# Decoder trunk on one core: the first slice of the lo half of each block's input in a tile of its own, 64 bytes further modulo 256

## The chip, the cores and the metric

The kernel runs on one core of one Trainium2 chip. The metric is the device time of one execution in microseconds (us). Before the change the median of three runs is 1512.07 us.

## What is computed

Two layers, each a SwiGLU feed-forward block (FFN), a token mixer with three branches, and a second FFN, on 256 tokens of width 1024. The reference, cut to its large products:

```python
for l in range(DEPTH):                       # DEPTH = 2
    g = norm_g[l]
    f = swiglu(rmsnorm(h, g[0]), w_ffn_gu[l, 0], w_ffn_down[l, 0])   # 1024 -> 2*2816 -> 1024
    h = h + 0.5 * rmsnorm(f, g[1])
    xn = rmsnorm(h, g[2])
    z = xn @ w_in[l]                         # 1024 -> 9224 columns
    ...
    merged = (gates[..., 0, :] * (y_m @ w_branch[l, 0])
              + gates[..., 1, :] * (y_s @ w_branch[l, 1])
              + gates[..., 2, :] * (y_x @ w_branch[l, 2]))
    y = merged @ w_out[l]
    h = h + rmsnorm(y, g[3])
    f = swiglu(rmsnorm(h, g[4]), w_ffn_gu[l, 1], w_ffn_down[l, 1])
    h = h + 0.5 * rmsnorm(f, g[5])
```

## The kernel before

**Products.** Every large product is taken to fp32 accuracy with three fp32r matmuls: each operand is split into a rounded half (hi, h) and the rest (lo, l), and hi·hi, hi·lo and lo·hi are summed in PSUM. `load_split` (L108 to L116) streams the weights: SyncE issues a DMA of 512 KB into `raw` (4 buffers), ScalarE casts `hi` (L114), VectorE subtracts to get `lo` (L115); `hi` and `lo` have 6 buffers each.

**The input of a block.** `split_x` (L174) makes the normalised, transposed input of an FFN or a mixer: for each of the 8 slices `kt` of 128 input channels ScalarE writes a slice of `xh` (L166) and VectorE a slice of `xl` (L167), each 128 x 256 (channels x tokens). It runs six times in the program, once for each of the two FFNs and the mixer of both layers. The slices lie one behind the other in one tile for `xh` and one for `xl`, so a slice starts 1024 bytes after the one before it.

**Transposed products.** `pair_T` (L191) loads 256 weight columns and makes two chains of matmuls (`cols_T`, `product`), each for 128 output columns:

```python
for (ah, al), (bh, bl) in terms:            # terms: kt = 0..7
    for u, v in ((ah, bh), (ah, bl), (al, bh)):
        nc.tensor.matmul(o, u, v, start=(i == 0), stop=(i == n - 1))   # L185
```

A chain is 24 matmuls: for each kt the weight slice hi with the moving operand `xh`, hi with `xl`, lo with `xh`; the weights are stationary (128 x 128), the input moves 256 columns. A call of `pair_T` is 48 matmuls at L185; the text calls it a block. The trace writes moving and stationary operand as `o<-xl,hi`. The program has 144 blocks with `xh` and `xl`: 22 in each of the four FFNs and 28 in each mixer. Blocks with other inputs (`ymh`/`yml`, `ysh`/`ysl`, `yxh`/`yxl` for the branches, `mh`/`ml` for the memory and the merged branches) are made by the same lines.

**Row products.** Where the result is wanted with tokens on the partitions, `rows_mm` (L198) takes the weights as the moving operand, 512 columns, and a 128 x 128 piece of the input as the stationary one (L203 hi, L204 lo, L205 with the lo half of the input). `group_rows` does this with `xh`/`xl`, `full_rows` for the FFN's second product with `hh`/`hl`; in the trace the moving operand again stands first (`acc<-hi,hh`, `o<-hi,xl`).

**Order.** An FFN goes over j = 0..10: two blocks with x (96 matmuls), then, from j = 1, two steps of the second product (`down`, 24 matmuls of 512 columns). The mixer mixes blocks, row products and small products by hand-written order. The order of the instructions on each engine is that in which the code is written.

**Where the tiles lie.** `TAGS` (L36) sets the size of each tile of the pool `act`, and so its start. `placed` (L118) takes a tile of that pool and views it as 8 slices. Bytes of SBUF in each partition, modulo 256: the weights `hi`, `lo` at 192, `xh` and `xl` at 128, `ymh`, `yml`, `ysh`, `ysl`, `yxh`, `yxl`, `mh`, `ml` at 128, `hh`, `hl` at 192.

Of the kernel before, what the change touches and what calls it, by code (L numbers as in the profile page):

```python
# [9 lines left out]
F32R = mybir.dt.float32r  # L10
# [4 lines left out]
P = 128  # L15
D = 1024
KT = D // P
S = 256
# [14 lines left out]
FREE = 4  # L33
BARE_TAIL = 3
BARE_FREE = 3
TAGS = {"xh": 2048, "xl": 2048, "qk": 2048, "vm": 2080, "vx": 2048, "yml": 2080, "kT": 2048, "ymh": 2048,  # L36
        "yxh": 2064, "yxl": 2096}
C_QK, C_V, C_O, C_I, C_F, C_U, C_SV, C_XQ, C_G = 0, 1024, 2048, 3072, 3076, 3080, 4104, 5128, 6152

# [2 lines left out]
def decoder_trunk(ctx: ExitStack, tc: tile.TileContext, x, mem, norm_g, w_ffn_gu, w_ffn_down, w_in, conv_w,  # L42
# [6 lines left out]
    act = ctx.enter_context(tc.tile_pool(name="act", bufs=1))  # L49
    tmp = ctx.enter_context(tc.tile_pool(name="tmp", bufs=2))  # L50
# [41 lines left out]
    def g_col(l, n, k):  # L92
        i = (l * 7 + n) * 8 + k
        return colA[:, i:i + 1]
# [13 lines left out]
    def load_split(src, a, b):  # L108
# [6 lines left out]
            nc.vector.tensor_tensor(out=lo, in0=raw, in1=hi.bitcast(F32), op=ALU.subtract)  # L115
        return hi, lo  # L116

    def placed(name, tag, dtype=F32R, at=0, n=KT * S):  # L118
        t = act.tile([P, TAGS[tag]], dtype, name=name, tag=tag)
        return t[:, at:at + n].rearrange("p (k s) -> p k s", s=S)  # L120
# [44 lines left out]
    def scaled_split(src, gain, hi, lo):  # L165
        last["act"] = nc.scalar.mul(hi, src, gain)  # L166
        last["dve"] = nc.vector.scalar_tensor_tensor(out=lo, in0=src, scalar=gain, in1=hi.bitcast(F32), op0=ALU.mult,  # L167
                                       op1=ALU.subtract)
# [3 lines left out]
        nc.vector.tensor_tensor(out=lo, in0=src, in1=hi.bitcast(F32), op=ALU.subtract)  # L172

    def split_x(l, n, pts):  # L174
        xh, xl = placed("xh", "xh"), placed("xl", "xl")
        for kt in range(KT):
            scaled_split(pts[kt // 2][:, kt % 2, :], g_col(l, n, kt), xh[:, kt, :], xl[:, kt, :])
        return xh, xl
# [56 lines left out]
    def boundary(accs, gb, mul, nxt, fill=(), lead=0):  # L235
# [28 lines left out]
        if lead:  # L264
            pts = new_pts()
            for tt in range(NT):
                transpose_in(xs[tt], tt, pts)
        xt = split_x(*nxt, pts)
        if not lead:
            hold[:] = [[]] * BARE_FREE + [[last["act"], last["dve"]]]  # L270
# [65 lines left out]
    def kv_parts(l):  # L336
        def start():
            mh, ml = placed("mh", "qk"), placed("ml", "vm")
            for kt in range(KT):
                scaled_split(memT[:, kt, :], g_col(l, 6, kt), mh[:, kt, :], ml[:, kt, :])  # L340
            vx = [act.tile([P, TAGS[t]], F32R, name="vx", tag=t)[:, 0:NT * D].rearrange("p (t d) -> p t d", d=D)
                  for t in ("vx", "yml")]
            kv[l] = ((mh, ml), [placed("kT", t) for t in ("kT", "ymh")], vx)

        def k_part(c):
            mt, kT, vx = kv[l]
            o = pair_T(w_mkv[l], c * 2 * P, mt)
            split(o, kT[0][:, 2 * c:2 * c + 2, :], kT[1][:, 2 * c:2 * c + 2, :])

        os_ = {}  # L350

        def v_quarter(c, q):
            mt, kT, vx = kv[l]
            os_[c] = group_rows(w_mkv[l], D + c * 512, mt, (q,), os_.get(c))
            if q == 3:
                for tt, o in enumerate(os_[c]):
                    split(o, vx[0][:, tt, c * 512:(c + 1) * 512], vx[1][:, tt, c * 512:(c + 1) * 512])

        return start, ([lambda c=c: k_part(c) for c in range(4)] +
                       [lambda c=c, q=q: v_quarter(c, q) for c in range(2) for q in range(4)])  # L360

    def mixer(l, xt, nxt, start=None, fill=(), lead=0):
# [55 lines left out]
        def attend(hd, pT):  # L418
# [7 lines left out]

        vm = act.tile([P, TAGS["vm"]], F32, name="vm", tag="vm")[:, 0:NT * NH * (DV + 1)].rearrange(
            "p (t h d) -> p t h d", t=NT, h=NH)
# [257 lines left out]
    transpose_in(xs, 1, pts)  # L686
    load_consts(rowA, colA, 112)
    xt = split_x(0, 0, pts)
    hold[:] = [[first], [], [last["act"], last["dve"]]]
    xt = ffn(0, 0, xt, (0, 2), {2: load_mem, 4: transpose_mem, 6: start0}, kv0, 3)  # L690
# [32 lines left out]
```

## Time and profile before

| | |
|---|---|
| median of 3 runs | 1512.07 us (1512.06 to 1513.64) |
| the profiled execution | 1514.27 us |
| its span in the trace | 1512.5 us |
| granted TensorE clock | 0.998 of 2.4 GHz |
| TensorE (PE) busy | 1493.2 us, 10870 matmuls |
| VectorE (DVE) busy | 929.3 us |
| ScalarE (ACT) busy | 749.0 us |
| DMA | 273.49 MB, 181 GB/s in the mean |

The span runs from the first to the last instruction that the profiler saw; the 1.8 us by which the execution is longer lie around it. A matmul's record in the trace is longer than the distance to the next one's start, since matmuls are pipelined: 276 to 283 ns stand in the record where the next starts after some 115 ns. What a matmul costs the engine is read from the distance of starts, or from the length of a piece of the chain of waits divided by its count.

### The profile page before, as it was taken

The numbers are of one execution on the slowest core, as the hardware profiler recorded it, in microseconds if no ns is written. First come the engines' busy times: TensorE is split into PE (matmuls) and PEld (weight loads), VectorE is DVE, ScalarE is ACT, GpSimd is POOL, SyncE is SP. The second block draws the span as 40 slices with busy tenths as digits, with TensorE's granted clock in tenths as the row PEclk, the third lists the DMA queues.
The fourth block names the chain that finished last, engine by engine and source line by source line (L and its number), as shares of the span: only waits on it lengthen the run. The fifth ranks groups of instructions, "written<-read, shape, count | busy, mean of one in ns | idle before, by whom it ended". The sixth has DMA issues, their size and how long they took to land.

```text
span 1512.5 us, 26330 instructions
## 1 busy us (share of the span) xinstructions
PE 1493.2 (99%) x10870; PEld 1410.2 (93%) x10870; DVE 929.3 (61%) x1319; ACT 749.0 (50%) x972; POOL 44.6 (3%) x77
## 2 busy tenths in 40 slices
PE   7999999999999999999999999999999999899998
PEld 7999998999999999999989999898998999799997
DVE  5564575777766567545465554576867665655454
ACT  6554464655444456444464444565544444454442
POOL 1000000000010000000000000000001000000000
PEclk9999999999999999999999999999999999999999
DMA  8666566455566565666656666655555656465662
GB/s 265 215 184 191 186 204 182 134 159 164 156 190 188 175 195 184 193 195 184 192 175 213 185 194 182 188 168 155 155 166 169 193 170 186 134 221 184 192 184 84
DMA packets 222169, 273.49 MB, mean 181 GB/s; under 512 B 12656, under 2 KB 194144, under 8 KB 222048
## 3 DMA queue, kind: packets, MB, share of 16 engines
q1 hardware_dynamic: 221920, 271.75, 59.4%
q8 instruction: 85, 1.39, 0.4%
q14 instruction: 36, 0.29, 0.1%
q10 hardware_dynamic: 128, 0.06, 0.0%
HBM read 270.72 MB, written 1.05 MB: 180 GB/s over the span
## 4 chain that ended last, share of the span: by engine, by line
PE 96%; DVE 2%; POOL 1%; DMA 0%; ACT 0%; issue 0%; SPq 0%; POOLq 0%; DVEq 0%; ACTq 0%
PE o L185 65%; PE acc L203 6%; PE acc L205 6%; PE acc L204 6%; PE o L203 3%; PE o L205 3%; PE o L204 3%; PE pts L159 1%; DMA raw<-in_w_ffn_gu_dram 0%; PE mx L647 0%; DVE lo L115 0%; PE zif L185 0%; POOL rs L142 0%; POOL rs L593 0%; ACT xh L166 0%
## 5 line engine op out<-in xcount | busy, mean ns | idle before, releaser
L115 DVE TENSOR_TENSOR lo<-raw,hi 128x1024 fp32r<-128x1024 f32 x504 | 614.0, 1222 | 493.0 <-ACT hi L114 483.6
L114 ACT CAST hi<-raw 128x1024 fp32r<-128x1024 f32 x504 | 527.4, 1050 | 600.9 <-PE o L185 279.4
L185 PE MATMUL o<-xh,hi 128*128 128x256 f32 x2304 | 650.6, 283 | 0.9 <-ACT xh L166 0.8
L185 PE MATMUL o<-xl,hi 128*128 128x256 f32 x2304 | 647.7, 281 | 0.4 <-DVE xl L167 0.3
L185 PE MATMUL o<-xh,lo 128*128 128x256 f32 x2304 | 647.1, 281 | 0.0
L185 PEld LDWEIGHTS o<-xh,lo 128*128 128x128 f32 x2304 | 440.2, 191 | 0.1
L185 PEld LDWEIGHTS o<-xh,hi 128*128 128x128 f32 x2304 | 434.6, 189 | 3.6 <-ACT xh L166 1.6
L185 PEld LDWEIGHTS o<-xl,hi 128*128 128x128 f32 x2304 | 435.1, 189 | 3.1 <-DVE xl L167 1.2
L203 PE MATMUL acc<-hi,hh 128*128 128x512 f32 x352 | 137.0, 389 | 0.0
L205 PE MATMUL acc<-hi,hl 128*128 128x512 f32 x352 | 136.8, 389 | 0.0
L204 PE MATMUL acc<-lo,hh 128*128 128x512 f32 x352 | 136.8, 389 | 0.0
L205 PEld LDWEIGHTS acc<-hi,hl 128*128 128x128 f32 x352 | 66.1, 188 | 13.9 <-DVE hl L172 0.2
L203 PEld LDWEIGHTS acc<-hi,hh 128*128 128x128 f32 x352 | 66.1, 188 | 12.5 <-ACT hh L171 0.3
L204 PEld LDWEIGHTS acc<-lo,hh 128*128 128x128 f32 x352 | 66.1, 188 | 12.2
L203 PE MATMUL o<-hi,xh 128*128 128x512 f32 x128 | 50.6, 395 | 0.0
L205 PE MATMUL o<-hi,xl 128*128 128x512 f32 x128 | 50.4, 394 | 0.0
L204 PE MATMUL o<-lo,xh 128*128 128x512 f32 x128 | 50.0, 391 | 0.0
L142 POOL TENSOR_TENSOR rs<-ms,mhalf 128x1 f32<-128x1 f32 x26 | 16.3, 627 | 1057.3 <-DVE ms L139 1057.3
L171 ACT CAST hh<-hf 128x512 fp32r<-128x512 f32 x44 | 27.4, 622 | 27.7 <-DVE hf L289 27.7
L185 PE MATMUL o<-yxh,hi 128*128 128x256 f32 x128 | 36.2, 283 | 0.0
L185 PE MATMUL o<-mh,hi 128*128 128x256 f32 x128 | 36.1, 282 | 0.0
L185 PE MATMUL o<-mh,lo 128*128 128x256 f32 x128 | 36.0, 281 | 0.0
(240 smaller groups left out, 1707.8 us busy)
## 6 DMA issues: line engine op xcount, KB each, us to landing
raw<-in_w_ffn_gu_dram SPq DMA_DIRECT2D x176, 512.0 KB, 4.7
raw<-in_w_in_dram SPq DMA_DIRECT2D x144, 512.0 KB, 3.7
raw<-in_w_ffn_down_dram SPq DMA_DIRECT2D x88, 512.0 KB, 4.4
raw<-in_w_branch_dram SPq DMA_DIRECT2D x48, 512.0 KB, 3.5
raw<-in_w_mkv_dram SPq DMA_DIRECT2D x32, 512.0 KB, 4.6
raw<-in_w_out_dram SPq DMA_DIRECT2D x16, 512.0 KB, 4.4
gb<-in_norm_g_dram SPq DMA_DIRECT2D x6, 512.0 KB, 4.4
h<-in_x_dram SPq DMA_DIRECT2D x4, 256.0 KB, 3.4
```

The costliest lines, as they stand in the source:

```text
L114: nc.scalar.copy(hi, raw)
L115: nc.vector.tensor_tensor(out=lo, in0=raw, in1=hi.bitcast(F32), op=ALU.subtract)
L142: nc.gpsimd.tensor_tensor(out=rs, in0=ms, in1=mhalf, op=ALU.pow)
L159: nc.tensor.transpose(out=pts[kt // 2][:, kt % 2, tt * P:(tt + 1) * P], in_=xs[kt // 4][:, kt % 4 * P:(kt % 4 + 1) * P], identity=ident)
L171: nc.scalar.copy(hi, src)
L185: nc.tensor.matmul(o, u, v, start=(i == 0), stop=(i == n - 1))
L203: nc.tensor.matmul(o, a, u, start=first, stop=False)
L204: nc.tensor.matmul(o, a, v, start=False, stop=False)
L205: nc.tensor.matmul(o, b, u, start=False, stop=last)
```

## The change

`split_x` takes its tiles from a new helper, `apart_x`. `xh` is as before. Of `xl` the slice kt = 0 goes into a tile `x0` of its own (pool `tmp`, one buffer), and the seven others into the `act` tile `xl`, which is smaller by one slice. `Slices` lets `cols_T` and `rows_mm` index both as before.

```diff
-TAGS = {"xh": 2048, "xl": 2048, "qk": 2048, ...
+TAGS = {"xh": 2048, "xl": 1792, "qk": 2048, ...
...
+    class Slices:
+        def __init__(self, parts):
+            self.parts = parts
+
+        def __getitem__(self, i):
+            return self.parts[i[1]][:, i[2]]
+
+    def apart_x():
+        zero = tmp.tile([P, S], F32R, name="x0", tag="x0", bufs=1)
+        rest = act.tile([P, TAGS["xl"]], F32R, name="xl", tag="xl")
+        return placed("xh", "xh"), Slices([zero] + [rest[:, k * S:(k + 1) * S] for k in range(KT - 1)])
...
     def split_x(l, n, pts):
-        xh, xl = placed("xh", "xh"), placed("xl", "xl")
+        xh, xl = apart_x()
```

The addresses that follow, in bytes in each partition, from the two built programs:

| tile | before | after | modulo 256 before | after |
|---|---|---|---|---|
| `xh` | 105088 | 112256 | 128 | 128 |
| `xl`, slices 1 to 7 | 113280 + 1024 kt | 105088 + 1024 (kt - 1) | 128 | 128 |
| `xl`, slice 0 (`x0`) | 113280 | 206016 | 128 | 192 |
| weights `hi`, `lo` | | unchanged | 192 | 192 |
| the other `act` tiles behind them | | 1024 lower | | unchanged |

No instruction is added, taken away or moved: with names and line numbers set aside the sequence of instructions of each engine, with what each waits for, is the same in both programs (PE 10798 rows, DVE 1321, ACT 907, POOL 82, SP 538). What changes is the address that one matmul in each chain of 24 reads its moving operand from (the second of the chain, `xl` of kt = 0), the address that 16 matmuls of `group_rows` load their stationary operand from, and the one that VectorE writes that slice to.

## Rows read from the trace of the kernel before

**Rows 1.** Page, parts 1 to 3: busy engines; granted clock by slice; share of DMA.
```profile
PE 1493.2 (99%) x10870; PEld 1410.2 (93%) x10870; DVE 929.3 (61%) x1319; ACT 749.0 (50%) x972; POOL 44.6 (3%) x77
...
PEclk9999999999999999999999999999999999999999
...
q1 hardware_dynamic: 221920, 271.75, 59.4%
```

**Rows 2.** Page, part 4: the chain that ended last, share by engine.
```profile
PE 96%; DVE 2%; POOL 1%; DMA 0%; ACT 0%; issue 0%; SPq 0%; POOLq 0%; DVEq 0%; ACTq 0%
```

**Rows 3.** What PE waited for: us in total, times, longest.
```profile
PE pts L159 <- DVE xs L153: 6.9, 3, 4.2
PE pt L89 <- DMA rowA<-in_norm_g_dram: 4.4, 1, 4.4
```

**Rows 4.** Page, part 5: groups by line: count, busy us, mean ns, idle before.
```profile
L115 DVE TENSOR_TENSOR lo<-raw,hi 128x1024 fp32r<-128x1024 f32 x504 | 614.0, 1222 | 493.0 <-ACT hi L114 483.6
...
L185 PE MATMUL o<-xl,hi 128*128 128x256 f32 x2304 | 647.7, 281 | 0.4 <-DVE xl L167 0.3
...
L203 PE MATMUL o<-hi,xh 128*128 128x512 f32 x128 | 50.6, 395 | 0.0
...
L204 PE MATMUL o<-lo,xh 128*128 128x512 f32 x128 | 50.0, 391 | 0.0
```

**Rows 5.** PE's groups by line, 434.84 to 450.6 us (first mixer).
```profile
L185 PE MATMUL o<-xl,hi 128*128 128x256 f32 x31 | 8.6, 276 | 0.0
...
L185 PE MATMUL o<-yml,hi 128*128 128x256 f32 x16 | 4.4, 276 | 0.0
```

**Rows 6.** The same view, 505.1 to 550.3 us (first mixer, later).
```profile
L185 PE MATMUL o<-xl,hi 128*128 128x256 f32 x64 | 18.0, 281 | 0.0
```

**Rows 7.** The chain of waits in order of time: start us, length us, what.
```profile
44.15 11.31 PE o L185 x96
60.89 11.31 PE o L185 x96
...
434.30 16.34 PE o L185 x144
...
505.10 45.23 PE o L185 x384
...
793.46 21.79 PE o L185 x192
...
1483.91 11.31 PE o L185 x96
```

**Rows 8.** Timeline of PE at 434 us, a block after a row product: start, record us.
```profile
434.14 0.28 PE L185 MATMUL o<-xh,hi 128*128 128x256 f32 x1
...
434.84 0.28 PE L185 MATMUL o<-xh,hi 128*128 128x256 f32 x1
...
435.18 0.28 PE L185 MATMUL o<-xh,hi 128*128 128x256 f32 x1
```

**Rows 9.** Timeline of PE at 44 us, the first block after a `down`.
```profile
43.98 0.28 PE L185 MATMUL o<-xh,hi 128*128 128x256 f32 x1
...
44.34 0.28 PE L185 MATMUL o<-xh,hi 128*128 128x256 f32 x1
```

**Rows 10.** Timeline of PE at 1344 us, the first `down` matmuls after a slow block.
```profile
1344.31 0.40 PE L203 MATMUL acc<-hi,hh 128*128 128x512 f32 x1
...
1345.01 0.39 PE L203 MATMUL acc<-hi,hh 128*128 128x512 f32 x1
...
1345.69 0.39 PE L203 MATMUL acc<-hi,hh 128*128 128x512 f32 x1
```

**Rows 11.** Timeline of PE at 38.5 us, the first `down` matmuls after a fast block.
```profile
38.53 0.39 PE L203 MATMUL acc<-hi,hh 128*128 128x512 f32 x1
...
39.22 0.39 PE L203 MATMUL acc<-hi,hh 128*128 128x512 f32 x1
...
39.90 0.39 PE L203 MATMUL acc<-hi,hh 128*128 128x512 f32 x1
```

More of the change, by code (lines that the diff above doesn't have):

```diff
@@ L35 @@
 BARE_FREE = 3
-TAGS = {"xh": 2048, "xl": 2048, "qk": 2048, "vm": 2080, "vx": 2048, "yml": 2080, "kT": 2048, "ymh": 2048,
+TAGS = {"xh": 2048, "xl": 1792, "qk": 2048, "vm": 2080, "vx": 2048, "yml": 2080, "kT": 2048, "ymh": 2048,
         "yxh": 2064, "yxl": 2096}
```

## The prediction

> **What bounds the kernel now.** I read the page's busy times first: TensorE is busy 99% of the span at full granted clock, VectorE 61%, ScalarE 50%, and the DMA engines are taken for 59% of it [rows 1]. Then the chain that ended last: 96% of it is TensorE [rows 2]. Then TensorE's waits: the two largest add up to 11.3 us, and both lie at a transpose, not in a product [rows 3]. So time can come only from the distance at which matmuls follow each other. L185 with `xh` and `xl` is the largest group, three forms of 2304 each [rows 4].
>
> Next I asked whether that distance is the same everywhere. It isn't. In the chain of waits, pieces of 96 matmuls without an interruption take 11.31 us, 117.8 ns each; there are 37 of exactly this length, from 44.15 to 1483.91 us, 36 of them with x [rows 7]. But 144 of the same matmuls take 16.34 us at 434.30, 113.5 ns each, and 192 at 793.46 take 21.79, also 113.5 [rows 7]. Grouped by line, the record of the same form is 276 ns in the one kind of stretch and 281 in the other [rows 5, 6]. Nothing waits in either, the clock is the same, the addresses are the same [rows 1, 5, 6]. The timeline shows how a pace starts. After a row product the block at 434.14 needs 0.70 us for its first six matmuls, unevenly, and from 434.84 three take 0.34 us, 113.3 ns each [rows 8]. The block at 43.98 takes 0.36 us for its first three [rows 9], evenly, and stays slow. A pace is kept through whole blocks and changes only where another kind of matmul comes between. Going through the program by starts I count, of the 144 x blocks, 120 slow, 2 half and half, 22 fast; of the `ym` and `ys` blocks, which follow x blocks, 14 slow and 2 fast.
>
> Of the entries into a block that begin unevenly, as at 434.14, I found eleven (around 96, 315, 324, 338, 434, 793, 993, 1056, 1066, 1080 and 1175 us), and all eleven settled at the fast pace within four to six matmuls. The slow pace was always entered without any unevenness. That is what the forecast rests on: slow looks like a stable beat that a disturbance ends.
>
> **The change, part by part.**
>
> *The instructions.* None is added or moved, so nothing new is issued, queued or waited for on any engine, SP's queue and POOL included. VectorE writes slice 0 with the same instruction to another address: nothing. The other `act` tiles move by 1024 bytes and keep their place modulo 256: nothing.
>
> *The second matmul of every chain* reads its moving operand at 192 modulo 256, where its stationary one lies too, instead of 128. The trace has no such matmul of 256 columns. The nearest rows are those where the kind of operand changes between neighbours: the first `down` matmul after a block, whose moving weights are at 192. At 1344.31 three of these take 0.70 us, against 0.68 for three a little later [rows 10]: the shift gives an uneven step, and then a settled pace. So I take it as a disturbance in each chain, 288 in all (144 blocks of two).
>
> *What a disturbance costs.* At 434.14 six matmuls take 0.70 us where the fast pace needs 0.68, so 0.02 us [rows 8]; the first three after 1344.31 lose 0.02 too [rows 10]. As bounds I take 0.01 and 0.045 us (nothing smaller shows in stamps of 10 ns; 0.045 is twice the rows). Taken: 0.025, so 288 x 0.025 = 7.2 us.
>
> *What it gives, if each chain then settles at the fast pace.* 117.8 - 113.3 = 4.5 ns a matmul. 122 slow blocks (the two halves counted as slow, which is small) x 48 x 4.5 ns = 26.3 us. The 14 `ym` and `ys` blocks take over the pace of the x block ahead, as `yml` does at the fast one [rows 5] and the four `ys` blocks in the slow piece of 384 at 505.10 do, which holds four x blocks too [rows 7]: 14 x 48 x 4.5 ns = 3.0 us.
>
> *`down` after fast blocks.* After a slow block `down` is mostly in its own beat at once (1344.31 is one of two exceptions); after a fast one its first three matmuls take 0.69 us where the next three take 0.68 [rows 11], 0.015 by the finer stamps, and 40 such entries would cost 0.6 us.
>
> *`group_rows`* loads `x0` as the stationary operand, 16 times, at 192 like the moving weights. The records of its forms with `xh` lie at 391 and 395 ns [rows 4]; 4 ns on all 384 would be 1.5 us either way. I take nothing, for I see no sign in it.
>
> *What must keep up.* A turn of the FFN takes 16.74 us (44.15 to 60.89) [rows 7] and needs six weight tiles, of which VectorE's subtraction at 1222 ns [rows 4] takes 7.3 us. With 0.4 us less a turn neither that nor the transfers, whose share would rise from 59% to 60% of the span, becomes the bound. Were that cover gone, the gain in the FFNs, about 88 of the 144 blocks, would shrink, not turn.
>
> The sum: -26.3 - 3.0 + 7.2 + 0.6 = -21.5 us. Against the profiled execution, 1514.27 us, that is 1492.8; the median of the runs is 2.2 us lower, so 1491 us there. With the bounds of the disturbance (2.9 to 13 us) and of `group_rows` the case itself spans 1485 to 1498.
>
> A rule of the Trainium skill speaks against any effect: the page "SBUF — State Buffer", section "Who interferes with whom", gives TensorE two independent read ports, one for the moving operand and one for weight loads, and says that TensorE never waits for anyone. By that the place of a slice could not matter, and the time would be 1512 us. The trace shows that the same matmul has two paces with no wait recorded [rows 5, 6], which that section doesn't explain; it does not show that addresses make them. The rule stands as the second rival.
>
> **The rivals.**
>
> *The disturbance settles slow: slower.* Every chain gets its uneven step, but the second matmul sits inside a chain, not at an entry, and the step may put it back into the slow beat each time. Then the 22 fast x blocks are lost, 22 x 48 x 4.5 ns = 4.8 us, with the 2 fast `ym` blocks 0.4 us, and 288 steps of some 8 ns (between 0 and the 0.02 of rows 10) cost 2.3 us: +7.5, 1519.5 us. For it: some 16 entries in the mixer whose first step alone is long (behind a small product) are slow from the second matmul on, and after slow blocks most `down` entries show no uneven step. Against it: the eleven. The point that decides: a chain gained is worth 24 x 4.5 ns = 0.108 us, and 44 chains are fast now; to pay for 288 steps of 0.025 us, 67 more must be, so with fewer than 111 of 288 chains fast the kernel is slower.
>
> *Nothing happens: 1512 us.* The address doesn't matter, or the shift is absorbed without a step. For it: most `down` entries, which also change from 128 to 192, show none. Against it: the exceptions, of which rows 10 is one, and that after a fast block the uneven step is regular [rows 11].
>
> *Half of it.* Only chains that start at some points of the beat are thrown into the fast pace, say half: half of the forecast's 21.5 us, about 1502 us.
>
> **How the numbers follow.** I give the forecast 0.48, the half effect 0.12, no effect 0.15, settling slow 0.25. Faster by over 0.2% (3 us, about what a measurement of this kernel can tell from no change): 0.48 + 0.12 = 0.60; within it 0.15; slower 0.25. The range goes from 1484, the low end of the likeliest case, to 1520, which takes in the slower rival's middle and leaves out less than 2 in 10. The likeliest case's own range is 1485 to 1498.
>
> **What would show it.** Right: the pieces of 96 at L185 take about 10.9 us instead of 11.31 (96 x 113.3 ns = 10.88, plus two steps of 0.025), the mean record of `o<-xl,hi` falls from 281 towards 276, three matmuls from the seventh of a chain on take 0.34 us, and the 505.10 piece of 384 takes about 43.7 instead of 45.23. The disturbance: the starts around the second matmul of each chain are uneven. Wrong: pieces of 96 at 11.31 or above; or a fast beat that the second chain of a block loses again; or a gain in L185 that comes back as waits for `lo` at L115.

## The result, and the profile after

The change makes the kernel faster by 1.0%: 1497.82 us median of four runs (1497.21 to 1498.27) against 1512.82 us before (median of four, the three on record and one more), ratio 0.9899 with a 95% interval of 0.9884 to 0.9915. The forecast of 1491 us was 6.8 us too low; the sign and the range were right. The profiled execution took 1498.12 us, its span 1496.4, which is 16.1 less than before. Lines behind the helper have moved down: L185 is now L197, L203 to L205 are L215 to L217. Parts 1, 3 and 4 of the page after:

```profile
PE 1477.0 (99%) x10870; PEld 1393.7 (93%) x10870; DVE 929.9 (62%) x1319; ACT 749.7 (50%) x972; POOL 44.6 (3%) x77
...
q1 hardware_dynamic: 221920, 271.75, 57.9%
...
PE 97%; DVE 1%; DMA 1%; ACT 0%; POOL 0%; issue 0%; SPq 0%; DVEq 0%; POOLq 0%; ACTq 0%
```

TensorE lost 16.2 us of busy time, the same as the span; VectorE and ScalarE did what they did in [rows 1]. The kernel is bound as before, and what changed is the distance between matmuls. Part 5 after, whose `o<-x,hi` is the displaced slice:

```profile
L197 PE MATMUL o<-xl,hi 128*128 128x256 f32 x2016 | 560.4, 278 | 0.3 <-DVE xl L179 0.3
...
L197 PE MATMUL o<-x,hi 128*128 128x256 f32 x288 | 81.6, 283 | 0.0
```

The record of the undisplaced form fell from 281 ns [rows 4] to 278, towards the 276 of a fast stretch [rows 5], while the displaced matmul itself has the longest record, 283. It is no faster for lying elsewhere; the others are. The chain of waits after (start us, length us):

```profile
43.81 11.00 PE o L197 x96
60.26 11.00 PE o L197 x96
...
500.44 43.75 PE o L197 x384
```

These answer to 11.31 at 44.15 and 45.23 at 505.10 [rows 7]. There are 36 pieces of 11.00 us. The piece of 384 is within 0.05 us of the 43.7 that was forecast; those of 96 take 11.00 where 10.9 was. A turn of the FFN went from 16.74 to 16.45 us. Where one chain follows another at the fast pace, the timeline shows the disturbance (start, record):

```profile
46.40 0.28 PE L197 MATMUL o<-xh,hi 128*128 128x256 f32 x1
46.52 0.28 PE L197 MATMUL o<-x,hi 128*128 128x256 f32 x1
46.63 0.28 PE L197 MATMUL o<-xh,lo 128*128 128x256 f32 x1
46.75 0.29 PE L197 MATMUL o<-xh,hi 128*128 128x256 f32 x1
46.88 0.28 PE L197 MATMUL o<-xl,hi 128*128 128x256 f32 x1
46.99 0.28 PE L197 MATMUL o<-xh,lo 128*128 128x256 f32 x1
```

From start to start, by the stamps in ns, the 179 such chains average 113.3, 119.2, 118.3, 124.2, 118.3 ns and then 113.3: four matmuls lose 26.7 ns together, and the fast pace is back. (The rows above are rounded to 10 ns and show this only in part.)

But not every chain settles. Classed by their second half, 243 of the 288 x chains are fast (46 before) and 45 slow: 38 that were slow and stay so, 7 that were fast. One of them, at 587 us:

```profile
587.34 0.28 PE L197 MATMUL o<-xh,hi 128*128 128x256 f32 x1
587.46 0.28 PE L197 MATMUL o<-x,hi 128*128 128x256 f32 x1
587.58 0.28 PE L197 MATMUL o<-xh,lo 128*128 128x256 f32 x1
...
590.17 0.28 PE L197 MATMUL o<-xh,hi 128*128 128x256 f32 x1
```

The next chain starts 2.83 us later, 24 x 117.9 ns; the displaced matmul moves a step or two by a few ns (118, 121, 114 instead of 117.8 each) and the slow pace goes on.

Paired matmul by matmul with the trace before, the 16.1 us come from these groups:

| group | predicted us | measured us |
|---|---|---|
| x blocks | -19.1 | -14.2 |
| `ym` and `ys` blocks | -3.0 | -3.0 |
| `down` | +0.6 | +0.5 |
| `group_rows` with x | 0 (1.5 either way) | +0.3 |
| all else | 0 | +0.4 |

Not all of the 14.2 us need be the change's. In every trace the first block, from about 12 us on, has matmuls some 213 ns apart for a while, whatever the kernel (here after the change; the granted clock of 12.2 to 18.7 us is recorded as 1.00):

```profile
14.95 0.41 PE L197 MATMUL o<-xl,hi 128*128 128x256 f32 x1
15.16 0.41 PE L197 MATMUL o<-xh,lo 128*128 128x256 f32 x1
```

Over the traces of this case that block takes between 8.4 and 10.9 us, 10.01 before and 9.55 after. Without it the x blocks gained 13.8 us. What makes and what ends this stretch no run here shows; where single traces are compared below, a difference of about 1 us can come from it.

### The profile page after: what moved, and what is told of

It reads as the page before. It is cut to its first block, busy times and chain, and to the rows that moved or that the text cites. A ratio compares the mean times of both kernels' runs of the same rounds, so it can differ in the third digit from the quotient of the medians.

```text
span 1496.4 us, 26330 instructions
## 1 busy us (share of the span) xinstructions
PE 1477.0 (99%) x10870; PEld 1393.7 (93%) x10870; DVE 929.9 (62%) x1319; ACT 749.7 (50%) x972; POOL 44.6 (3%) x77
## 4 chain that ended last, share of the span: by engine, by line
PE 97%; DVE 1%; DMA 1%; ACT 0%; POOL 0%; issue 0%; SPq 0%; DVEq 0%; POOLq 0%; ACTq 0%
PE o L197 65%; PE acc L216 6%; PE acc L215 6%; PE acc L217 6%; PE o L215 3%; PE o L216 3%; PE o L217 3%; PE pts L171 1%; DMA raw<-in_w_ffn_gu_dram 1%; PE mx L659 0%; PE zif L197 0%; DVE lo L115 0%; POOL rs L605 0%; ACT xh L178 0%; PE pt L424 0%; PE pt L615 0%
## 5 line engine op out<-in xcount | busy, mean ns | idle before, releaser
L197 PE MATMUL o<-xh,hi 128*128 128x256 f32 x2304 | 645.7, 280 | 0.9 <-ACT xh L178 0.7
L197 PE MATMUL o<-xh,lo 128*128 128x256 f32 x2304 | 641.2, 278 | 0.0
L197 PE MATMUL o<-xl,hi 128*128 128x256 f32 x2016 | 560.4, 278 | 0.3 <-DVE xl L179 0.3
L197 PEld LDWEIGHTS o<-xh,hi 128*128 128x128 f32 x2304 | 434.4, 189 | 3.5 <-ACT xh L178 1.6
L197 PEld LDWEIGHTS o<-xh,lo 128*128 128x128 f32 x2304 | 434.6, 189 | 0.1
L197 PEld LDWEIGHTS o<-xl,hi 128*128 128x128 f32 x2016 | 380.6, 189 | 0.7 <-DVE xl L179 0.7
L215 PE MATMUL acc<-hi,hh 128*128 128x512 f32 x352 | 137.1, 390 | 0.0
L217 PE MATMUL acc<-hi,hl 128*128 128x512 f32 x352 | 137.0, 390 | 0.0
L197 PE MATMUL o<-x,hi 128*128 128x256 f32 x288 | 81.6, 283 | 0.0
L217 PEld LDWEIGHTS acc<-hi,hl 128*128 128x128 f32 x352 | 66.1, 188 | 14.1 <-DVE hl L184 0.2
L215 PEld LDWEIGHTS acc<-hi,hh 128*128 128x128 f32 x352 | 66.1, 188 | 12.6 <-ACT hh L183 0.3
L197 PEld LDWEIGHTS o<-x,hi 128*128 128x128 f32 x288 | 54.8, 190 | 1.9 <-DVE x L179 0.2
L215 PE MATMUL o<-hi,xh 128*128 128x512 f32 x128 | 50.8, 397 | 0.0
L217 PE MATMUL o<-hi,xl 128*128 128x512 f32 x112 | 43.8, 391 | 0.0
L197 PE MATMUL o<-yxh,hi 128*128 128x256 f32 x128 | 36.2, 283 | 0.0
```

The source lines that it names most:

```text
L215: nc.tensor.matmul(o, a, u, start=first, stop=False)
L217: nc.tensor.matmul(o, b, u, start=False, stop=last)
```

## The experiments

After the result the theory was this. The slow pace is a beat of three matmuls (117.5, 117.5 and 118.3 ns in turn, as means over chains of the trace before by the stamps in ns), the fast one has only one step. A matmul whose operand lies out of line with its neighbours pushes the beat; whether it ends fast depends on which of the three places it falls on. 24 is a multiple of three, so a slice keeps its place from chain to chain. The trace of before bears this out looking back: of the slow x chains whose long distance stood behind the third matmul of each kt, all 184 became fast; where it stood behind the second, 28 of 32 stayed slow; behind the first, 10 of 26. Each kernel below was measured against the kernel before; its ratio and interval stand with it. Where a run needs room, some small tiles get 2 or 3 buffers instead of 4, and the sizes of tiles in `TAGS` are set so that the others keep their place modulo 256; most of these lines are not shown below.

**A tile of its own, not displaced.** From the changed kernel:

```diff
-        zero = tmp.tile([P, S], F32R, name="x0", tag="x0", bufs=1)
+        zero = act.tile([P, S], F32R, name="x0", tag="x0")
```

> Slice 0 of xl in a tile of its own, but at 128 modulo 256 like the others. If the 64 bytes make the disturbance: the time of before, 1512 us, 46 of the 288 x chains fast, pieces of 96 at 11.31 us. Rival, the gain comes from the new tile or from xl and xh having changed places: about 1498 us, as with the change.

Measured: 1513.03 us, ratio 1.0004 (0.9994 to 1.0013). The pieces of 96 in the chain of waits are as long as before:

```profile
43.16 11.31 PE o L197 x96
59.90 11.31 PE o L197 x96
```

The tile alone gives no gain, nor does it that `xh` and `xl` changed places; the 64 bytes make it. 58 of 288 chains were fast here where 46 had been: 8 of the 12 more begin the last FFN. How a block is entered varies a little from one program to another, or from one execution to another; which was not tried.

**Slice 4 instead of slice 0.**

```diff
-        return placed("xh", "xh"), Slices([zero] + [rest[:, k * S:(k + 1) * S] for k in range(KT - 1)])
+        parts = [rest[:, k * S:(k + 1) * S] for k in range(KT - 1)]
+        return placed("xh", "xh"), Slices(parts[:4] + [zero] + parts[4:])
```

> Slice 4 of xl displaced by 64 bytes instead of slice 0 (14th matmul of the chain instead of the 2nd). Theory: the slow beat repeats every three matmuls (117.5, 117.5, 118.3 ns), 2 and 14 stand at the same place in it, so the same 45 chains stay slow that stay slow with the change; the some 80 chains that are entered slow run 12 matmuls longer at the slow pace, 80 x 12 x 4.5 ns = 4.3 us: 1502 us. Rival, where the kick comes is a new draw each time: another set of slow chains, 20 to 100 of them, 1498 to 1506.

Measured: 1497.71 us, ratio 0.9903 (0.9887 to 0.9920); the pieces of 96 are 11.05 us long, 36 of them:

```profile
43.02 11.05 PE o L198 x96
```

26 chains stay slow to their end, 24 of them among the 45; two are new (at 349.27 and 1037.91 us) and 21 got out, so the expected set came only in part. The place in the beat can be read better here than anywhere else, since a chain runs 13 matmuls before it meets the displaced slice. Of the chains that arrive there in a steady slow beat, by the stamps in ns, all 53 with the long distance behind the third matmul of each kt end fast, and all 24 with it behind the second (16) or the first (8) stay slow, the two new ones among them. (Left out are the program's first chain, one with a pause in it, and three at the start of the last FFN that run interleaved.)

The time missed the 1502. x blocks took 804.65 us against 804.30 with the change; without the first block, 795.94 against 794.75. I had put the chains that are entered slow and settle at 80; there were 53, 53 x 12 x 4.5 ns = 2.9 us of delay, and the 21 gave a part of it back.

**Slice 0 of `xh` instead of `xl`.**

```diff
-TAGS = {"xh": 2048, "xl": 1792, ...
+TAGS = {"xh": 1792, "xl": 2048, ...
...
+        rest = act.tile([P, TAGS["xh"]], F32R, name="xh", tag="xh")
+        return Slices([zero] + [rest[:, k * S:(k + 1) * S] for k in range(KT - 1)]), placed("xl", "xl")
```

> Slice 0 of xh displaced by 64 bytes instead of that of xl: the 1st and the 3rd matmul of the chain, the two other places in the beat of three. Theory: the 45 chains that the change leaves slow get out of the slow beat (28 of the 32 that had the long distance at the 2nd place stayed slow), while two disturbances per chain cost up to twice 0.027 us: 45 x -0.1 + 243 x (0 to 0.027) = -4.5 to +2 us against the change, 1493 to 1500. Rival, it doesn't matter which matmul is displaced: the same chains slow, 1498 to 1504.

Measured: 1497.57 us, ratio 0.9901 (0.9886 to 0.9916). The time lies in the expected range, but by luck: new slow chains were not expected. Of the 45 chains 35 are fast now, and 44 others are slow: all 35 that come right behind a `down`, of which the change had none, and 9 in the mixers. Three chain starts in a turn of the FFN, of this kernel:

```profile
42.31 0.28 PE L197 MATMUL o<-x,hi 128*128 128x256 f32 x1
...
45.14 0.28 PE L197 MATMUL o<-x,hi 128*128 128x256 f32 x1
...
47.88 0.28 PE L197 MATMUL o<-x,hi 128*128 128x256 f32 x1
```

The first chain takes 2.83 us, slow to its end, the next 2.74. With the change the same two chains started at 43.64, 46.40 and 49.15 us: 2.76 and 2.75. So it matters which matmul is displaced, and the rival (any matmul serves alike) falls. This kernel displaces two matmuls of a chain, not one, so it does not separate their number from their place; that the place in the beat decides rests on the run with slice 4. The time is the same as the change's because 35 chains are won and 44 lost, and the chains that settle behind a slow one pay 25 ns here, where those that settle behind a `down` pay 38 with the change. In a fast chain the two displaced matmuls together cost 26.7 ns, no more than the one did.

**Once per turn in the FFNs.** A copy of slice 0 at 128 modulo 256 for the other three chains:

```diff
+        if twin:
+            xl.twin = Slices([act.tile([P, TAGS["yxh"]], F32R, name="x1", tag="yxh")[:, :S]] + rest)
...
+        if xl.twin:
+            last["dve"] = nc.vector.tensor_copy(xl.twin[:, 0, :], xl[:, 0, :])
...
-            cols_T(o[:, m, :], wt, m * P, xt)
+            t = getattr(xt[1], "twin", None)
+            cols_T(o[:, m, :], wt, m * P, (xt[0], t) if t and (m or calm) else xt)
```

> In the FFNs only the first of the four chains of a turn reads the displaced slice; the other three read a copy of slice 0 at 128 modulo 256 (one more VectorE instruction per FFN). The mixers as with the change. Theory: the fast pace holds without a disturbance, and each disturbance left out saves 0.027 us: 132 x 0.027 = 3.5 us less than with the change, 1494.3 us; pieces of 96 behind the first turn at about 10.92 us. Rival, the fast pace needs the disturbance in each chain: the three other chains of a turn fall back to 117.8 ns, 132 x 0.108 - 3.5 = +11 us, 1509.

Measured: 1494.72 us, ratio 0.9877 (0.9860 to 0.9893), 35 pieces like this one:

```profile
43.75 10.92 PE o L205 x96
```

The fast pace holds by itself, and a disturbance costs about what was worked out: the x blocks took 800.64 us against 804.30, 3.7 less where 3.5 was expected (791.29 against 794.75 without the first block, 3.5 less). The single try can fail: four turns stayed slow in all four chains, the one at 94.73 us among them (11.54 us). With the change four turns were slow throughout too, one of them the same. In the mixers, where this run changed nothing, 10 chains turned fast and 6 slow: so many can change sides from one program to another with no cause in the edit.

```profile
94.73 11.54 PE o L205 x96
```

**Other distances.** Slice 0 of `xl` at 0 and at 64 modulo 256 (a tile of 320 columns, read from column 16 or 32; two small tiles with 3 buffers instead of 4 make room):

```diff
-        zero = tmp.tile([P, S], F32R, name="x0", tag="x0", bufs=1)
+        zero = tmp.tile([P, S + 64], F32R, name="x0", tag="x0", bufs=1)[:, 32:32 + S]
```

> Slice 0 of xl at 0 modulo 256, 128 bytes further than the rest instead of 64. If any matmul out of line disturbs the beat: about as the change, 1494 to 1502, with another set of slow chains. If only the place where the weights lie does: near before, 1510 to 1514.

> Slice 0 of xl at 64 modulo 256, 192 bytes further (or 64 back). If any matmul out of line disturbs the beat: 1494 to 1502, with another set of slow chains. If only the place where the weights lie does: 1510 to 1514.

Measured: at 0, 1517.41 us, ratio 1.0030 (1.0019 to 1.0041); at 64, 1493.44 us, ratio 0.9870 (0.9850 to 0.9890). Pieces of the chain of waits, at 0 first:

```profile
43.54 11.31 PE o L197 x96
...
434.56 16.89 PE o L197 x144
```

```profile
43.53 10.98 PE o L197 x96
```

At 0 the disturbance ends slow: 271 of 288 chains, 40 of the 46 fast ones lost; the 144 matmuls that took 16.34 us before [rows 7] take 16.89. At 64, 276 are fast and 12 slow, and a fast chain loses 19.9 ns instead of 26.7. The expectations had either any displacement serve or only that to the place of the weights. At 64 the first came nearly true, at 0 neither did: the two kernels differ in nothing but the size of the displacement, and it decides which way the beat is pushed.

**All slices elsewhere.** From the kernel before, all of `xh` and `xl` at 192 (here), and at 64 (160 in place of 128, 16 in place of 48):

```diff
-    colA = act.tile([P, 112], F32, name="colA")
+    colA = act.tile([P, 128], F32, name="colA")[:, :112]
...
-TAGS = {"xh": 2048, "xl": 2048, ...
+TAGS = {"xh": 2048, "xl": 2048 + 48, ...
```

> From the kernel before: all of xh and xl at 192 modulo 256, where the weights lie, no slice apart. Theory of the disturbance alone: no matmul differs from its neighbours, both paces stay as they are, 1512 us give or take 5. Rival, it is the place relative to the weights that sets the pace (FFN down, both at 192, runs 226.7 ns for 512 columns, that is 113.3 for 256): every x chain fast without any disturbance, 1512 - 26 - 3 = 1483 us.

> From the kernel before: all of xh and xl at 64 modulo 256, no slice apart. The run with all at 192 had one pace, 120.0 ns, whatever came before a block: the place relative to the weights sets which paces there are. Expected: again a pace of its own, the same in all x chains, between 113.3 ns (1483 us) and 120 (1530). Rival: the paces of 128, both of them, 1512.

Measured: 1529.97 us at 192, the median of three executions, ratio 1.0117 (1.0100 to 1.0134), where a fourth took 4237.72 us, of which no trace was kept, and is left out; and 1528.61 at 64, ratio 1.0102 (1.0082 to 1.0123). A piece of each:

```profile
44.50 11.51 PE o L185 x96
```

```profile
42.83 11.52 PE o L185 x96
```

No x chain is fast in either; at 192 they settle at 120.0 ns, all alike, at 64 at 118.3 to 120.3, where one pace was expected. The `ym` and `ys` blocks, whose operands stayed at 128, are all fast (113.3 ns), and the 14 x chains right behind them run at 120.0 at 192 and 118.7 at 64: a fast pace ahead is not kept there. So the place of the moving operand, with the weights at 192, decides which paces appear at all, and of the three places tried only 128 showed the fast one. Neither side of the first expectation held: 512 columns run fast with both operands at 192 (226.7 ns), 256 columns don't. All slices at 0, and other places of the weights, were not tried, so whether it is the distance of the two that counts stays open.

**Put together.** Slice 0 at 64 and, in the FFNs, once per turn; then also slice 0 of `ml` displaced by 64 bytes:

```diff
-            mh, ml = placed("mh", "qk"), placed("ml", "vm")
+            mh, mv_ = placed("mh", "qk"), act.tile([P, TAGS["vm"]], F32R, name="ml", tag="vm")
+            ml = Slices([mv_[:, 7 * S + 16:8 * S + 16]] + [mv_[:, k * S:(k + 1) * S] for k in range(KT - 1)])
```

> Both gains together: slice 0 of xl at 64 modulo 256 (1493.4 us, a disturbance of a fast chain costs 19.9 ns there) and, in the FFNs, only in the first chain of a turn. 132 disturbances of 0.020 us less: 2.6 us, so 1490.8 us. Rival: with the disturbance in the first chain alone more turns stay slow, because a second try is missing: 1492 to 1497.

> As the run before it, and slice 0 of ml 64 bytes further modulo 256 too (at 192), so that the 16 chains with mh and ml, all at 117.8 to 118.3 ns until now, are disturbed as well. If they settle fast: 16 x (24 x 4.5 - 27) ns = 1.3 us less than e10. If they stand in the slow beat where the disturbance leaves it: no change.

Measured: 1492.24 us (1490.57 to 1492.51), ratio 0.9859 (0.9844 to 0.9874), and 1490.82 us (1490.42 to 1491.43), ratio 0.9851 (0.9834 to 0.9867). Two pieces of 96 of the first of them:

```profile
44.80 10.92 PE o L205 x96
...
95.77 11.54 PE o L205 x96
```

Of the 2.6 us that the first was to gain on 1493.44, 1.2 came. In the profiled execution the first turns ended 1.3 us later (44.80 against 43.53); 1.2 of it is the first block, which took 10.87 us against 9.68, and without it the x blocks took 788.96 us against 790.92, 2.0 less. One turn, at 95.77, stayed slow in all four chains because its only try failed, 0.5 us: the rival, in one place. With `ml`, 12 of the 16 chains are fast instead of 2, 44.47 us instead of 45.20, 0.7 of the 1.3 us that were expected. The intervals of the two overlap, so that they differ is not shown; that both are faster than before by 1.4 to 1.5% is, and the last is 7 us under the change.

## Why the prediction was right, and where it was not

*What bounds the kernel, and that the gain would not come back elsewhere*: right. TensorE's busy time and the span fell by the same 16 us, and the waits after are as before, 6.9 and 4.3 us for the two largest against 6.9 and 4.4 [rows 3]:

```profile
PE pts L171 <- DVE xs L165: 6.9, 3, 4.2
PE pt L89 <- POOL z L454: 4.3, 1, 4.3
```

*That a displaced slice disturbs the beat, and that this is what helps*: right, by the run with the slice in a tile of its own but not displaced (1513.03 us).

*The price, 0.025 us a disturbance*: right for a chain that was fast (0.0267 by the trace; 3.7 us for 132 of them by the run with one per turn). A slow chain that settles pays more, 0.038 us; one that stays slow pays nothing.

*The `ym` and `ys` blocks take over the pace ahead of them*: right in the sum, -3.0 us, all 32 chains fast. As a reason it is too narrow: with `xh` and `xl` at 192 the same 32 chains are fast behind x blocks that are not. *`down`*: right, +0.5 for +0.6.

*"What it gives, if each chain then settles at the fast pace"*: this is the term that was too large. 243 of 288 chains settle. Worked again with the counts: 204 gained, 204 x 24 x 4.45 ns = 21.8 us; 7 lost, 0.7; 243 disturbances at a mean of 29 ns, 7.0. That is -14.1 us for the x blocks, where the trace has -14.2 (-13.8 without the first block) and the sum had -19.1. That the 7.0 is so near to the forecast's 7.2 is luck: fewer chains paid than the 288, and those that settle out of the slow pace paid more than 25 ns. The median's 15.0 us is a little less than the 16.1 of the profiled pair, for the execution profiled before was above its median.

The flaw was in the evidence. The eleven uneven entries that all ended fast all began at a chain's first matmul, and I took the slow pace for a beat without places. It has three, and the fine stamps of before show which of them a chain stands in; read that way they would have split the slow chains into 184 sure gains and 58 doubtful ones. The rival of half an effect named this ("chains that start at some points of the beat") but had its share wrong: it is 45 chains, not half. Its time of about 1502 us (1501 by its own working) is nearer to the measured 1497.8 than the forecast's 1491. That 1497.8 still lies within the 1485 to 1498 of the likeliest case is luck: the upper end came from disturbances of 0.045 us, not from chains that don't settle.

Two readings behind the forecast were also too strong. An uneven entry that ended slow had been missed: at 1320.88 us, where the last FFN starts, the first ten matmuls take 1.86 us, with steps from 0.12 to 0.34. And a pace can change inside a block, with no other kind of matmul between; in the trace before, a pause did it, and the chain that follows at 993.28 is fast:

```profile
992.36 0.28 PE L185 MATMUL o<-xh,hi 128*128 128x256 f32 x1
992.95 0.38 PE L185 MATMUL o<-xl,hi 128*128 128x256 f32 x1 [0.31 <-DVE xl L167]
```

*The slower rival* (the disturbance settles slow) did not happen with 64 bytes forward, but is real: at 128 bytes forward it gave 1517.41 us, where the rival's own working had 1519.5. That this distance was the good one is luck: nothing in the trace of before told the two apart.

*The second rival*, from the Trainium skill ("SBUF — State Buffer", section "Who interferes with whom": two independent read ports, TensorE waits for nobody), falls as far as one concludes from it that a place cannot matter, as the prediction did: the same matmul ran at 113.3, 117.8 and 120.0 ns with nothing but the place of its operand and the beat it was entered in changed. What in the machine makes the beat no run here shows.

## What to carry to other kernels

Where TensorE is the bound and the same matmul shows two distances in one trace, read the distances in ns and look at how each pace is entered and left; a few per cent lie there that no instruction count shows. Try the place modulo 256 of the moving operand first as a whole (here 128 was the only one of three that showed a fast pace, and the others cost 1.0 to 1.2%), then one slice out of line, several distances and positions, since the wrong distance cost 0.3% where the right one brought 1.3%. A pace once reached held here until another kind of matmul or a pause came, so one disturbance behind each change of the kind of matmul mostly does it (it failed in 4 of 44 FFN turns at 64 bytes forward), and each further one cost 0.02 to 0.03 us.

## What was not expected of the hardware

- A matmul that reads its moving operand 64 bytes out of line can change the pace of the 22 that follow it, and that of the next blocks until another kind of matmul comes, by 4.5 ns each.
- The same displacement works or not by the place in a beat of three matmuls: with slice 4 displaced, 53 of 53 chains with the long distance behind the third matmul settle fast, none of 24 with it elsewhere. And 35 of 35 chains behind a `down` settle with the second matmul of the chain displaced, none of the 35 with the first and third.
- With all of `xh` and `xl` 64 bytes further (192) or back (64) no x chain is fast: 120.0 ns a matmul at 192, where 512 columns with both operands at 192 keep 226.7 ns.
